# Moving the fifth bias table of a neighbourhood attention stage behind the first token tile's steps on GpSimd's queue

## The chip, the cores and the metric

One core of one Trainium2 chip runs the whole program. The metric is the device time of one execution in microseconds (us); of the kernel before there are three timed runs and one execution that was taken with a profile. The engines are named as the profile names them: PE is TensorE's matmul side and PEld its weight loads, DVE is VectorE, ACT is ScalarE, POOL is GpSimd, and SP is SyncE, which here only issues transfers.

## What is computed

The reference is an encoder trunk of two layers over 256 tokens of width 1024, in float32:

```python
for layer in range(DEPTH):                     # DEPTH = 2
    x = x + 0.5 * swiglu(rms_norm(x, ffn1_norm[layer]), ...)
    h = rms_norm(x, mix_norm[layer])
    x = x + (even_mixer(h, ...) if layer % 2 == 0 else odd_mixer(h, w_qkv, rel_bias, w_out, rows))
    x = x + 0.5 * swiglu(rms_norm(x, ffn2_norm[layer]), ...)
return rms_norm(x, final_norm)
```

The change lies in the odd mixer of the second layer. It projects to queries, keys and values of 16 heads of 64, and each token attends to a window of its neighbours on a grid of 4 rows by 64 columns. A learned bias, `rel_bias`, which depends on the head and on the two offsets of row and column, is added to the scores ahead of the softmax, and positions outside the window get minus 1e30.

## The kernel before, in words

**Stages.** The program runs six stages one after the other: a feed-forward stage, the even mixer, two feed-forward stages, the odd mixer (`odd`, line 1085), and a last feed-forward stage. The 256 tokens are two tiles of 128 (`tt` 0 and 1). Weights come from memory in units of up to 1 MB by SP (`load`, line 312) into three raw buffers. ACT rounds each piece to a high part (`hi`, line 415), DVE takes the rest as a low part (`lo`, line 418), and PE makes three matmuls for each pair of pieces: high by high (line 407), low by high (line 408) and high by low (line 409). When both parts of a raw buffer have been made, SP's next transfer into it may start.

**How the order comes about.** Each engine carries out its instructions in the order in which the program writes them. The program writes the matmuls of the main loop, and behind each set of three it calls `tick` (line 232). A tick resumes the side tasks whose countdown has run out. A side task is a generator that writes some instructions, for any engine, and yields the number of ticks to its next piece. So a `yield` costs nothing on the chip by itself: it only decides where in the queues of the engines the next instructions stand.

**The odd mixer.** It works on two groups of eight heads. For each group the main loop projects keys, then queries, then values, for both token tiles. The results pass through these tasks:

- `natural` (line 1097) scales a projection on ACT (`nat`, line 1105; for queries DVE first makes the factor `rs`, line 1103) and has PE turn it into `tp` (`turned`, line 484).
- `stack_q` (line 496) writes the turned queries: high parts on ACT and low parts on DVE, both into `oqT`.
- `stack_k` (line 507) does the same for the keys of one token tile: high parts on ACT into `okTz`, low parts on DVE into half the partitions of `okTx`, and a copy of the high parts by POOL into the other half of `okTx` (the CAST of line 514). `okTz` and `okTx` exist twice, for head 0 and head 1 of each pair. Their other halves are cleared by POOL's memsets (line 521), which `keys_tiles` writes when a group begins.
- `attend` (line 762) takes a group's heads in steps `(tt, b0, s)`: tile 0 with `b0` 0 and 2 and `s` 0 and 1, then tile 1. A step writes the scores on PE (`scores`, lines 830 and 831; line 831 reads `okTx`), then DVE adds the bias table and takes the maximum (line 848), ACT makes the exponentials (line 872), DVE normalises (lines 884 and 886), PE turns the result (line 894), and after two steps PE weighs the values (line 815). A score takes all 256 keys, so it needs the keys of both token tiles.

**Bias tables.** `bias_tables` (line 1065) makes eight tables on POOL, one for each two heads, four to a group; the table of number `n` is made in two halves (line 1077) out of rows of `rel_bias` that SP has fetched (`fetch_row`, line 1051). Four row buffers exist, filled for tables 0 to 3 in the stage before; the rows of table `n + 4` are asked for behind table `n`, when its buffer is free. So the rows of the fifth table, `n` = 4, are asked for on SP's queue, which also carries the weights. Five table buffers exist, hence the `while`: table `n` from 5 on may only be written when the four steps that read table `n - 5` have been written. `read` counts these steps as the program writes them. `BIAS_GAP` is the number of ticks behind each half, 0 for tables 0 to 3 and 3 for the others; a number up to 1 means the next tick.

Of the kernel before, what the change touches and what calls it, by code (L numbers as in the profile page):

```python
# [166 lines left out]
class Trunk:  # L167
# [897 lines left out]
    def bias_tables(self, rel, tables, read):  # L1065

        nc = self.nc
        yield BIAS_WAIT
        for n in range(8):
            while n >= 5 and read[n - 5] < 4:  # L1070
                yield 1
            bias = self.t([P, 2, 6, GRID_W], "bias", 5)
            for i in range(2):
                row = self.rows[n][:, i, :]
                runs = bass.AP(row.tensor, row.offset, [row.ap[0], [31, 6], [1, GRID_W]])
                near = self.near.unsqueeze(1).to_broadcast([P, 6, GRID_W])
                nc.gpsimd.tensor_tensor(bias[:, i], runs, near, op=ALU.add)
                if i == 0:
                    yield BIAS_GAP[n // 4]
            tables.append(bias)  # L1080
            if n + ROWS < 8:
                self.fetch_row(rel, n + ROWS)
            yield BIAS_GAP[n // 4]
# [239 lines left out]
```

## Time and profile before

| | us |
|---|---|
| three timed runs | 972.93, 973.35, 974.29 |
| median of these | 973.35 |
| the execution that was profiled | 974.63 |
| its span, from the first to the last instruction | 972.8 |
| PE busy in the span | 954.3 |
| DVE busy | 694.8 |
| ACT busy | 557.2 |
| POOL busy | 88.2 |

The mean granted clock of TensorE over the span is 0.995 of full speed. The odd mixer takes the stretch from some 655 to some 785 us of the span. In a row of the timeline the first number is the start in us, the second the duration, then engine, line, operation and tile; what stands in brackets is how long the engine had been idle just before and what ended that. A row with a count above 1 is merged out of several instructions that follow each other on the engine, and its second number is the time from the first start to the last end. A matmul's duration is modelled and longer than its share of the pipeline; the distance from one start to the next says what it cost.

### The profile page before, as it was taken

What the parts mean: (1) busy time and instruction counts of PE and PEld (TensorE: products, weight loads), DVE (VectorE), ACT (ScalarE), POOL (GpSimd) and SP (SyncE); (2) the same over time, 40 slices, a digit from 0 to 9 for tenths busy, and PEclk for the clock granted to TensorE, in tenths of its full rate; (3) what the DMA queues carried; (4) which work ended last, traced back from release to release, by engine and by line L of the source; (5) the groups of instructions that cost most, each with busy time, mean ns of one, the idle gap of its engine ahead of it and who ended that gap; (6) DMA issues with size and microseconds to landing.
All of it is one profiled execution on the core that took longest, in us unless ns stands there. A gap on an engine that the chain in (4) does not pass through costs nothing.

```text
span 972.8 us, 12839 instructions
## 1 busy us (share of the span) xinstructions
PE 954.3 (98%) x4803; PEld 806.5 (83%) x4803; DVE 694.8 (71%) x1104; ACT 557.2 (57%) x965; POOL 88.2 (9%) x152
## 2 busy tenths in 40 slices
PE   9999999999999999999999999999899999999997
PEld 6888998877778889988888899887678788889886
DVE  5665679778966665787755558788577776655987
ACT  7554556477776544554645546556677575545551
POOL 1030000063410000000000000004230000000002
PEclk9999999999999999999999999999899999999999
DMA  8565555644326645557465465655333456555641
GB/s 271 197 240 187 178 212 181 209 130 106 112 91 218 212 152 159 209 217 255 135 215 193 139 210 189 216 178 187 106 130 130 130 180 210 183 155 182 212 172 71
DMA packets 82367, 171.64 MB, mean 176 GB/s; under 512 B 3712, under 2 KB 25216, under 8 KB 82304
## 3 DMA queue, kind: packets, MB, share of 16 engines
q1 hardware_dynamic: 81728, 170.23, 52.7%
q8 instruction: 37, 0.61, 0.3%
q10 hardware_dynamic: 576, 0.59, 0.2%
q14 instruction: 26, 0.21, 0.1%
HBM read 169.76 MB, written 1.05 MB: 176 GB/s over the span
## 4 chain that ended last, share of the span: by engine, by line
PE 89%; DVE 4%; ACT 2%; DMA 1%; POOL 1%; issue 1%; POOLq 0%; SPq 0%; ACTq 0%; DVEq 0%
PE pj L407 14%; PE pj L409 13%; PE pj L408 13%; PE s L409 11%; PE s L407 11%; PE s L408 11%; PE tp L484 3%; PE o L815 2%; PE o L408 1%; PE o L407 1%; PE o L409 1%; DVE lo L418 1%; PE tp L894 1%; PE tp L462 1%; PE s L830 1%
## 5 line engine op out<-in xcount | busy, mean ns | idle before, releaser
L418 DVE TENSOR_TENSOR lo<-raw,hi 128x1024 fp32r<-128x1024 f32 (+2 forms) x388 | 382.5, 1009 | 121.7 <-ACT hi L415 118.3
L415 ACT ACTIVATE hi<-raw 128x1024 fp32r<-128x1024 f32 (+2 forms) x388 | 327.9, 877 | 148.0 <-PE pj L409 103.9
L407 PE MATMUL pj<-hi,th 128*128 128x512 f32 (+1 forms) x512 | 198.8, 388 | 0.0
L409 PE MATMUL pj<-hi,tl 128*128 128x512 f32 (+1 forms) x512 | 193.6, 378 | 0.0
L408 PE MATMUL pj<-lo,th 128*128 128x512 f32 (+1 forms) x512 | 193.3, 378 | 0.1
L407 PE MATMUL s<-hi,th 128*128 128x512 f32 (+1 forms) x400 | 152.5, 381 | 0.0
L409 PE MATMUL s<-hi,tl 128*128 128x512 f32 (+1 forms) x400 | 149.8, 374 | 0.0
L408 PE MATMUL s<-lo,th 128*128 128x512 f32 (+1 forms) x400 | 149.5, 374 | 0.0
L409 PEld LDWEIGHTS pj<-hi,tl 128*128 128x128 f32 x512 | 96.5, 188 | 15.6
L407 PEld LDWEIGHTS pj<-hi,th 128*128 128x128 f32 x512 | 96.8, 189 | 13.9 <-issue 0.9
L408 PEld LDWEIGHTS pj<-lo,th 128*128 128x128 f32 x512 | 96.8, 189 | 13.5 <-DVE lo L418 0.5
L409 PEld LDWEIGHTS s<-hi,tl 128*128 128x128 f32 x400 | 75.5, 189 | 11.1
L408 PEld LDWEIGHTS s<-lo,th 128*128 128x128 f32 x400 | 75.6, 189 | 10.6
L407 PEld LDWEIGHTS s<-hi,th 128*128 128x128 f32 x400 | 75.7, 189 | 10.3
L599 DVE SCALAR_TENSOR_TENSOR glu<-pj,rstd,silu 128x512 f32<-128x512 f32 (+1 forms) x48 | 33.7, 701 | 36.8 <-PE pj L409 36.6
L418 DVE TENSOR_TENSOR g_l<-tp,g_h 128x384 fp32r<-128x384 f32 (+1 forms) x48 | 29.0, 604 | 22.2 <-ACT g_h L415 22.2
L427 POOL TENSOR_TENSOR rstd<-var,mhalf 128x1 f32<-128x1 f32 (+2 forms) x16 | 15.2, 948 | 312.6 <-DVE var L425 312.5
L447 ACT ACTIVATE th<-tp,mats 128x128 fp32r<-128x128 f32 x88 | 25.1, 371 | 31.3 <-PE tp L462 27.0
L407 PE MATMUL s<-hi,g_h 128*128 128x512 f32 (+1 forms) x108 | 42.8, 396 | 0.0
L409 PE MATMUL s<-hi,g_l 128*128 128x512 f32 (+1 forms) x108 | 42.0, 389 | 0.0
L415 ACT ACTIVATE g_h<-tp 128x384 fp32r<-128x384 f32 (+1 forms) x48 | 25.3, 526 | 29.1 <-PE tp L484 19.0
L408 PE MATMUL s<-lo,g_h 128*128 128x512 f32 (+1 forms) x108 | 41.9, 388 | 0.0
(378 smaller groups left out, 1383.1 us busy)
## 6 DMA issues: line engine op xcount, KB each, us to landing
raw<-in_ffn_w_down SPq DMA_DIRECT2D x44, 1024.0 KB, 5.0
raw<-in_ffn_w_up SPq DMA_DIRECT2D x32, 1024.0 KB, 5.2
raw<-in_ffn_w_gate SPq DMA_DIRECT2D x30, 1024.0 KB, 5.1
raw<-in_ffn_w_gate SPq DMA_DIRECT2D x16, 768.0 KB, 4.5
raw<-in_ffn_w_up SPq DMA_DIRECT2D x16, 768.0 KB, 4.7
raw<-in_odd_w_qkv SPq DMA_DIRECT2D x12, 1024.0 KB, 5.2
raw<-in_even_w_in SPq DMA_DIRECT2D x4, 1024.0 KB, 5.0
raw<-in_even_w_out SPq DMA_DIRECT2D x8, 512.0 KB, 5.7
```

The lines of the kernel that those rows point to most:

```text
L407: mm(ps, h, wh, start=first, stop=False)
L408: mm(ps, h, wl, start=False, stop=False)
L409: mm(ps, l, wh, start=False, stop=last)
L415: self.nc.scalar.activation(hi, src, AF.Copy)
L418: self.nc.vector.tensor_tensor(lo, src, hi.bitcast(F32), op=ALU.subtract)
L427: nc.gpsimd.tensor_tensor(r[:, :n], v[:, :n], self.mhalf[:, :n], op=ALU.pow)
L447: self.nc.scalar.activation(hi, tb[:, j * P : j * P + P], AF.Copy, scale=gain)
L462: nc.tensor.transpose(tb[:, j * P : (j + 1) * P], self.x[tt][:, b * P : (b + 1) * P], self.ident)
L484: self.nc.tensor.transpose(tb[:, i * P : (i + 1) * P], src[:, i * P : (i + 1) * P], self.ident)
L599: nc.vector.scalar_tensor_tensor(m[:, :w], u[:, :w], self.now.r[tt], s[:, :w], op0=ALU.mult, op1=ALU.mult)
L815: self.nc.tensor.matmul(O[64 * s : 64 * s + 64, i * P : i * P + P], v(b0 + i, s, kc), pT[s][:, i, kc, :], start=(kc == 0), stop=(kc == 1),)
L830: nc.tensor.matmul(S[:, i, :], q, kz[s], start=True, stop=False)
```

## The change

```diff
         nc = self.nc
         yield BIAS_WAIT
         for n in range(8):
-            while n >= 5 and read[n - 5] < 4:
+
+            while n >= 5 and read[n - 5] < 4 or n == 4 and read[1] < 2:
                 yield 1
             bias = self.t([P, 2, 6, GRID_W], "bias", 5)
             for i in range(2):
```

The fifth table is now written only when two steps that read table 1 have been written. Table 1 belongs to the second two heads of the first group's first steps; its first two readers are the steps `(0, 0, 0)` and `(0, 0, 1)`, those of token tile 0. Tables 5 to 7 keep their condition. One line is added ahead of it, so lines from 1071 on have a number larger by one.

On POOL the piece of the queue in which the fifth table stands reads as follows in the kernel before. `bias_6383` is the fourth table and `bias_6408` the fifth, made from `rows_6316`; the first two casts copy the keys of token tile 0 and the next two those of token tile 1; the memsets belong to the second group, and `bias_6819` is the sixth table.

```order
L427 TENSOR_TENSOR rstd_6389<-var_6387,mhalf_82 128x1
L1077 TENSOR_TENSOR bias_6383<-rows_5365,mats 128x384
L1077 TENSOR_TENSOR bias_6408<-rows_6316,mats 128x384
L514 CAST okTx_1466_6256<-okTz_1464_6254 64x4x128
L514 CAST okTx_1467_6257<-okTz_1465_6255 64x4x128
L1077 TENSOR_TENSOR bias_6408<-rows_6316,mats 128x384
L514 CAST okTx_1466_6256<-okTz_1464_6254 64x4x128
L514 CAST okTx_1467_6257<-okTz_1465_6255 64x4x128
L521 MEMSET okTz_1572_6693 64x1024
L521 MEMSET okTz_1573_6694 64x1024
L1077 TENSOR_TENSOR bias_6819<-rows_6335,mats 128x384 x2
```

In the changed kernel the same piece of POOL's queue is this, the fifth table being `bias_6653` now:

```order
L427 TENSOR_TENSOR rstd_6389<-var_6387,mhalf_82 128x1
L1078 TENSOR_TENSOR bias_6383<-rows_5365,mats 128x384
L514 CAST okTx_1466_6256<-okTz_1464_6254 64x4x128
L514 CAST okTx_1467_6257<-okTz_1465_6255 64x4x128
L514 CAST okTx_1466_6256<-okTz_1464_6254 64x4x128
L514 CAST okTx_1467_6257<-okTz_1465_6255 64x4x128
L1078 TENSOR_TENSOR bias_6653<-rows_6316,mats 128x384 x2
L521 MEMSET okTz_1572_6693 64x1024
L521 MEMSET okTz_1573_6694 64x1024
L1078 TENSOR_TENSOR bias_6819<-rows_6335,mats 128x384 x2
```

Both halves of the fifth table have moved behind all four casts and still stand ahead of the second group's memsets. Nothing else has moved on POOL, and PE, DVE, ACT and SP have the same instructions in the same order as before; the fifth table issues no transfer of its own.

On PE, unchanged, the first score (four matmuls of lines 830 and 831, of which the second is the first to read `okTx`) stands behind the query projection of token tile 1 and ahead of the value projection of tile 0; behind the first nine matmuls of that value projection stand the four that turn the queries of tile 1 (line 484).

## The prediction

> **What bounds the kernel now.** I read the page first, then who waited for whom on PE, then the clock in stretches around the longest wait, then the timeline of that place engine by engine.
>
> ```profile
> span 972.8 us, 12839 instructions
> PE 89%; DVE 4%; ACT 2%; DMA 1%; POOL 1%; issue 1%; POOLq 0%; SPq 0%; ACTq 0%; DVEq 0%
> ```
>
> The chain that ended last is PE's for 89% of the span, so the kernel is bound by PE, and what makes it shorter is either less PE work or less waiting by PE. The change removes no work. So the question is where PE waits:
>
> ```profile
> PE s L831 <- POOL okTx L514: 5.3, 1, 5.3
> PE o L1246 <- DVE zeros L1244: 1.5, 1, 1.5
> ```
>
> These are the two longest waits of PE in the whole execution. The first is one wait of 5.3 us: the first score of the odd mixer waits for POOL's cast. It is also followed by slow matmuls; in the stretches below the value behind the POOL column is the granted clock, a share of full speed.
>
> ```profile
> 679.40:685.20 5.80, 0.50 (x2) 0.19 (x1) 2.18 (x5) 1.72 (x3) 4.12 (x5) 0.87 0.31 60
> 685.20:690.10 4.90, 4.90 (x14) 3.92 (x15) 1.56 (x6) 0.00 (x0) 2.50 (x3) 0.50 0.87 279
> ```
>
> PE is busy for 0.50 us of the first 5.80, and in the 4.90 us behind it the clock stands at 0.50. Why POOL is late, its own timeline shows, with two pieces of the chain of waits behind it:
>
> ```profile
> 667.60 0.94 POOL L1077 TENSOR_TENSOR bias<-rows,mats 128x384 f32<-128x384 f32 x1
> 680.76 0.93 POOL L1077 TENSOR_TENSOR bias<-rows,mats 128x384 f32<-128x384 f32 x1 [12.21 <-DMA rows<-in_c_rel_bias]
> 681.75 1.72 POOL L514 CAST okTx<-okTz 64x512 fp32r<-64x512 f32 x2
> 683.55 0.93 POOL L1077 TENSOR_TENSOR bias<-rows,mats 128x384 f32<-128x384 f32 x1
> 684.54 1.27 POOL L514 CAST okTx<-okTz 64x512 fp32r<-64x512 f32 x2
> 685.87 1.95 POOL L521 MEMSET okTz<- 64x1024 f32 x2
> ```
>
> ```profile
> 674.62 0.61 SPq L1057
> 675.28 5.34 DMA rows<-in_c_rel_bias
> ```
>
> POOL has ended the fourth table at 668.54 (667.60 and 0.94). The next in its queue is the first half of the fifth, whose rows SP asks for only at 674.62 and which land 5.34 us on. So POOL stands idle for 12.21 us with the casts queued behind. Then a half, two casts, the other half, two casts; the first of the last two ends at 685.15 and PE starts at 685.20.
>
> **The change, part by part.** It removes and adds nothing. Two halves of 0.93 us go past four casts, on POOL alone; the fifth table asks for no rows, so SP's queue is as before.
>
> *When the casts run now.* They need the keys' high parts from ACT, of which those of tile 1 are the later:
>
> ```profile
> 670.22 1.21 ACT L415 ACTIVATE okTz<-tp 64x512 fp32r<-64x512 f32 x2 [1.21 <-PE tp L484]
> ```
>
> Tile 1's are there at 671.43. Tile 0's stand well ahead of them in ACT's queue, so its two casts (1.27 us) start when POOL is free, at some 668.6, and end by 669.9. How fast casts follow, the second group's keys show, where nothing is ahead of them:
>
> ```profile
> 713.64 1.21 ACT L415 ACTIVATE okTz<-tp 64x512 fp32r<-64x512 f32 x2 [2.02 <-PE tp L484]
> 714.36 1.28 POOL L514 CAST okTx<-okTz 64x512 fp32r<-64x512 f32 x2 [3.60 <-ACT okTz L415]
> 714.88 1.39 DVE L418 TENSOR_TENSOR okTx<-tp,okTz 64x512 fp32r<-64x512 f32 x2 [2.20 <-ACT okTz L415]
> ```
>
> The casts end 2.00 us after ACT's start, so at 672.22 here. PE reaches the score at 679.59: POOL is 7 us early, and the wait goes.
>
> *What is late next at the score.* It also needs DVE's low parts of the queries, the first at 678.76, two in 1.41 us:
>
> ```profile
> 678.76 1.41 DVE L418 TENSOR_TENSOR oqT<-tp,oqT 64x512 fp32r<-64x512 f32 x2
> 679.59 0.36 PE L830 MATMUL s<-okTz,oqT 128*128 128x256 f32 x1
> 685.20 0.58 PE L831 MATMUL s<-okTx,oqT 128*128 128x256 f32 x1 [5.26 <-POOL okTx L514]
> 689.85 0.95 PE L484 MATMUL tp<-mats,nat 128*128 128x128 f32 x4
> 690.55 0.48 PE L407 MATMUL pj<-hi,th 128*128 128x512 f32 x1
> ```
>
> That start at 679.59 stays. From it to 690.55 PE needs 10.96 us for four score matmuls, nine of the value projection and four that turn the queries of tile 1. Undisturbed, the same work costs what it does elsewhere in this stage:
>
> ```profile
> 693.42 0.28 PE L830 MATMUL s<-okTz,oqT 128*128 128x256 f32 x1
> 693.89 0.40 PE L407 MATMUL pj<-hi,th 128*128 128x512 f32 x1
> 695.96 0.39 PE L407 MATMUL pj<-hi,th 128*128 128x512 f32 x1
> ...
> 669.58 0.60 PE L484 MATMUL tp<-mats,nat 128*128 128x128 f32 x4
> 669.94 0.48 PE L407 MATMUL pj<-hi,th 128*128 128x512 f32 x1
> ```
>
> Start to start that is 0.47 for a score, 2.07 for nine matmuls (three sets lie between 693.89 and 695.96) and 0.36 for the turning, 2.90 together. So 10.96 - 2.90 = 8.06 us are to be had. Of these, 685.20 - 679.59 - 0.12 = 5.49 are the wait itself (0.12 being a quarter of 0.47), and the other 2.57 the slow clock.
>
> [...]
>
> *Whether the rest follows.* Behind the score, the next that PE needs from others is `nat` of the queries of tile 1, and the next that others need from PE is its turning:
>
> ```profile
> 681.07 0.69 ACT L1105 ACTIVATE nat<-pj,rs 128x512 f32<-128x512 f32 x1 [2.54 <-DVE rs L1103]
> 681.65 1.14 ACT L415 ACTIVATE hi<-raw 128x512 fp32r<-128x512 f32 x2
> 690.84 0.59 ACT L415 ACTIVATE oqT<-tp 64x512 fp32r<-64x512 f32 x1 [8.04 <-PE tp L484]
> ```
>
> PE now comes to the turning at 679.59 + 0.47 + 2.07 = 682.13, and `nat` ends at 681.76: 0.37 us to spare. ACT is through with its two pieces at 682.79 and then idled 8.04 us for PE, so its whole later queue comes forward by about as much as PE. On DVE the first score's maximum comes forward less:
>
> ```profile
> 682.31 0.69 DVE L418 TENSOR_TENSOR lo<-raw,hi 128x512 fp32r<-128x512 f32 x1 [1.35 <-ACT hi L415]
> ...
> 686.25 0.42 DVE L848 CUSTOM_DVE_ANT_1 p<-s,bias 128x256 f32<-128x256 f32 x1 [3.25 <-PE s L831]
> ```
>
> It starts at 683.0, behind that low part, 3.2 us earlier and not 8. Two maxima (about 0.9) and a low part (0.69) behind it end at 684.6, while ACT's parts of the queries of tile 1 are there at 682.8 + 1.2 = 684.0. So DVE is 0.6 us later against PE than before. PE doesn't read these queries before the scores of tile 1, over 20 matmuls on.
>
> The weights: one transfer starts at a time that does not move, all later ones are released by DVE's low parts, which come forward too.
>
> ```profile
> 683.03 0.37 SPq L322 DMA_DIRECT2D raw<-in_odd_w_qkv  x1
> ...
> 697.61 0.37 SPq L322 DMA_DIRECT2D raw<-in_odd_w_qkv  x1
> raw<-in_odd_w_qkv SPq DMA_DIRECT2D x12, 1024.0 KB, 5.2
> ```
>
> The first lands at about 683.03 + 5.2 = 688.2. Of the three raw buffers, the one that SP got at 697.61 held a unit two ahead of it, so its own first piece was split later than that; with 8 us off, later than 689.6. It is there in time.
>
> *What the move costs.* POOL's casts at 668.6 now run beside DVE's low parts of the weights. DVE, in the stretch in which POOL made tables (658.5 to 668.5) and in the one in which it stood idle (668.5 to 680.5):
>
> ```profile
> L418 DVE TENSOR_TENSOR lo<-raw,hi 128x512 fp32r<-128x512 f32 x5 | 5.7, 1165 | 0.3 <-ACT hi L415 0.3
> ...
> L418 DVE TENSOR_TENSOR lo<-raw,hi 128x512 fp32r<-128x512 f32 x8 | 5.3, 690 | 3.2 <-ACT hi L415 3.1
> ```
>
> A low part beside POOL's work took 0.475 us longer. Three of them stand where the first casts go:
>
> ```profile
> 668.56 1.90 DVE L418 TENSOR_TENSOR lo<-raw,hi 128x512 fp32r<-128x512 f32 x3
> 671.46 1.39 DVE L418 TENSOR_TENSOR okTx<-tp,okTz 64x512 fp32r<-64x512 f32 x2 [1.00 <-ACT okTz L415]
> ```
>
> At worst 3 x 0.475 = 1.43, of which DVE's idle 1.00 takes most; 0.43 is left, and it could go through `rs`, `nat` and the turning to the score at 679.59. At best nothing, since the casts last 1.3 us and not 1.9. The second pair of casts meets the keys' low parts, which take 1.39 us at 714.88 with casts beside them and 1.39 at 671.46 without. A gain by less contention later is possible as well, since the memsets leave 685.87; it would be off PE's path. I take 0.15.
>
> [...]
>
> The fifth table itself ends at 680.76 + 1.9 = 682.7, and the memsets at 684.7 (1.95 behind it), ahead of the 687.8 of before. Group 2 needs the memsets at 713.64 - 8 = 705.6, and reads the fifth table later still. Both are covered by over 20 us.
>
> **The sum.** 8.06 - 0.15 = 7.9 us. The profiled execution of 974.63 us (its span and 1.83 around it) becomes 966.7. It lies 1.28 above the median of the runs, 973.35, from which the same gain gives 965.5.
>
> **The rivals.** *Only the wait goes.* The runs without a profile lie up to 1.7 us below the profiled one; where the rows land sooner or the slow clock does not set in, there is less to gain. Then 5.49 less up to 0.43, so some 5.1 to 5.5 us: 968.0. The 0.50 over 4.90 us speaks against it.
>
> *A new wait takes part of the place.* `nat` has 0.37 us to spare and hangs on DVE's `rs`, behind queries' low parts that have none. If DVE runs late by one table half beside it (0.93) at two steps, PE waits up to 1.9 us less 0.37 there: 973.35 - 7.9 + 1.5 = 967.0. The half at 680.76 stands in the same place in both kernels, which speaks against it.
>
> *No change.* The score's wait was inferred from semaphores. Were it DVE's or the row transfer's own, the order on POOL would not matter: 973.4. The cast that ends at 685.15 and the start at 685.20 speak against it.
>
> *Slower.* The fifth table now stands directly ahead of the second group's memsets. If its rows came late, the memsets, then ACT's keys of the second group, then PE would wait. That costs PE something once the memsets end after 705.6, so when the rows land 21 us later than they did, and it makes the kernel slower by 2 us once they land 31 us later: 975.4. In the profile they took 5.34 us.
>
> **How the numbers follow.** The full gain has 0.72; its own range is 7.0 to 8.6 us, with half a microsecond for the median of other runs, 964.7 to 966.4. Only the wait 0.16, a new wait 0.05, no change 0.04, slower 0.03. Low end: 8.06 and about 1 for the scatter of the runs (972.93 to 974.29) gives 964.3. High end: the wait alone less contention and half a microsecond of scatter, 4.5, gives 968.9. What a measurement can tell from no change is about 0.2%, 1.95 us; the first three cases pass it: faster 0.93, same 0.04, slower 0.03.
>
> **What would show it.** In the profile of the changed kernel: no wait of PE for `okTx`; four casts ended by 673, both halves of the fifth table behind them from some 680.8; no stretch at clock 0.50 near 685; ACT's idle of 8.04 ahead of `oqT` under 0.5; a span of about 964.9. I am wrong if PE still waits over 1 us between 679 and 684, or if the 8 us come back as waits before the stage ends.

## The result, and the profile after

The changed kernel takes 965.62 us in the median (965.20 to 966.42 in four runs); the kernel before, with one more run beside its three from above, 973.14 (972.89 to 974.29). The ratio is 0.9921, with a 95% interval of 0.9904 to 0.9939: faster by some 7.5 us. The predicted time was 965.5.

From the page of the changed kernel and from what PE waited for, the longest first:

```profile
span 963.4 us, 12838 instructions
```

```profile
PE o L1247 <- DVE zeros L1245: 1.4, 1, 1.4
PE tp L970 <- POOL kra L923: 1.0, 1, 1.0
```

The wait of 5.3 us that headed this list is gone, and no other came in: what led behind it leads now. The two stretches that showed the idle PE and the slow clock, by the same columns as before:

```profile
679.40:685.20 5.80, 5.80 (x31) 4.87 (x30) 4.32 (x12) 5.45 (x10) 3.65 (x4) 1.00 0.37 118
685.20:690.10 4.90, 4.90 (x27) 4.20 (x26) 4.20 (x15) 4.87 (x12) 0.00 (x0) 1.00 0.69 189
```

PE is busy throughout and the clock stands at 1.00. POOL's queue at that place:

```profile
666.15 0.94 POOL L1078 TENSOR_TENSOR bias<-rows,mats 128x384 f32<-128x384 f32 x1
667.15 3.82 POOL L514 CAST okTx<-okTz 64x512 fp32r<-64x512 f32 x4
679.25 1.91 POOL L1078 TENSOR_TENSOR bias<-rows,mats 128x384 f32<-128x384 f32 x2 [8.27 <-DMA rows<-in_c_rel_bias]
681.21 1.95 POOL L521 MEMSET okTz<- 64x1024 f32 x2
```

All four casts have ended by 670.97. POOL still waits 8.27 us for the rows of the fifth table, but nothing that PE needs stands behind it. PE at the first score, up to the first matmul behind the turning of the second queries:

```profile
678.14 0.35 PE L830 MATMUL s<-okTz,oqT 128*128 128x256 f32 x1
678.33 0.28 PE L831 MATMUL s<-okTx,oqT 128*128 128x256 f32 x1
678.68 0.40 PE L407 MATMUL pj<-hi,th 128*128 128x512 f32 x1
...
680.77 0.60 PE L484 MATMUL tp<-mats,nat 128*128 128x128 f32 x4
681.13 0.48 PE L407 MATMUL pj<-hi,th 128*128 128x512 f32 x1
```

The score starts 1.45 us earlier in this execution than in that of before (679.59), and so does everything ahead of it: the fourth table's last half starts at 666.15 against 667.60. That offset is older than the place of the change. From the score to the last row PE took 681.13 - 678.14 = 2.99 us, where it had taken 10.96. So 7.97 us went here, and with the offset that is the whole difference of the two spans, 972.8 - 963.4 = 9.4. Nothing was given back later: from these last rows to the end of the span it is 282.27 us after and 282.25 before. By the medians the gain is 7.5 us and not 7.97; single runs of one kernel lie over 1 us apart.

### The profile page after: what moved, and what is told of

The parts are those of the page before. It is cut to its first block, busy times and chain, and to the rows that moved or that the text cites. A ratio compares the mean times of both kernels' runs of the same rounds, so it can differ in the third digit from the quotient of the medians.

```text
span 963.4 us, 12838 instructions
## 1 busy us (share of the span) xinstructions
PE 950.2 (99%) x4803; PEld 803.6 (83%) x4803; DVE 696.2 (72%) x1104; ACT 557.4 (58%) x965; POOL 87.5 (9%) x152
## 4 chain that ended last, share of the span: by engine, by line
PE 91%; DVE 4%; ACT 2%; POOL 1%; issue 1%; DMA 1%; POOLq 0%; ACTq 0%; DVEq 0%
PE pj L407 14%; PE pj L409 14%; PE pj L408 14%; PE s L407 12%; PE s L409 12%; PE s L408 11%; PE tp L484 3%; PE o L815 2%; PE o L409 1%; PE o L407 1%; PE o L408 1%; PE tp L894 1%; DVE lo L418 1%; PE tp L462 1%; PE s L830 1%
```

## The experiments

Each was timed beside the kernel before. In the three sessions that one had medians of 973.61, 973.34 and 973.60.

### The slow clock by itself

PE gets 22 matmuls that nobody reads, directly ahead of the first score of the kernel before. They use the high parts of the main loop's last set once more, which `mm` notes for them:

```diff
+        self.recent = lh[0], piece
...
+            if tag == "ot0_" and (tt, b0, s) == (0, 0, 0):
+                h, piece = self.recent
+                o = self.bank("o")
+                for _ in range(22):
+                    nc.tensor.matmul(o, h, piece.split.parts[0][:, piece.i, :], start=True, stop=True)
             S = self.scores(tt, b0, s, qT(tt), kT, sink is not None)
```

> The kernel before, with 22 extra matmuls on PE directly ahead of the odd mixer's first score; they write a free PSUM bank that nothing reads, so they only keep PE busy through most of its wait for POOL's casts (22 x 0.23 = 5.0 us of the 5.5). Theory (5.49 us of the 8 are the wait, 2.57 the slow clock behind it): the wait ends when it did, but the clock stays full, so 973.1 - 2.5 = 970.6 us, and no stretch at clock 0.50. Rival (the slow clock costs nothing by itself, or doesn't come from PE's idleness): 973.1, with the slow stretch still there or PE waiting for somebody else in its place.

Measured: 971.14 us, a ratio of 0.9974 (0.9965 to 0.9983), so 2.5 us less with more work. PE in this run (line numbers are larger by 1 to 6; 837 is the score's second matmul, 408 the first of a set):

```profile
678.41 5.15 PE L780 MATMUL o<-hi,th 128*128 128x512 f32 x22
683.40 0.28 PE L836 MATMUL s<-okTz,oqT 128*128 128x256 f32 x1
684.25 0.39 PE L837 MATMUL s<-okTx,oqT 128*128 128x256 f32 x1 [0.58 <-POOL okTx L515]
...
684.72 0.40 PE L408 MATMUL pj<-hi,th 128*128 128x512 f32 x1
684.95 0.40 PE L409 MATMUL pj<-lo,th 128*128 128x512 f32 x1
```

The casts come when they came before, and PE goes on no sooner; but its matmuls follow at 0.23 us behind the wait and not at 0.43. In the profile PE takes 2.89 us from the end of the wait to the first matmul behind the turning (684.25 to 687.14), where it had taken 5.35 (685.20 to 690.55). The slow clock was 2.5 of the 8 us, as the sum had it (2.57), and PE's own idleness made it.

### The wait, without moving anything

The kernel before with its order, but with the fifth table made from the fourth table's rows, which have long landed. So this kernel leaves out the fifth table's own values:

```diff
-                row = self.rows[n][:, i, :]
+                row = self.rows[3 if n == 4 else n][:, i, :]
...
-            if n + ROWS < 8:
+            if n + ROWS < 7:
                 self.fetch_row(rel, n + ROWS)
+            if n == 4:
+                self.fetch_row(rel, 7)
```

> The kernel before with its order on POOL untouched, but the fifth table is made from the fourth table's rows, which have long landed (so its values are not those of the reference); the fourth row buffer is refilled behind it. Theory (what costs is that the casts queue behind a table that waits for its rows, not the 1.9 us of the table itself): POOL no longer stands idle, the casts end by about 674, 5 us ahead of the score at 679.6, and the time is that of the change, 965.6 us. [...]

Measured: 966.52 us, 0.9928 (0.9914 to 0.9942). POOL, DVE and PE in this run:

```profile
667.42 1.84 POOL L1077 TENSOR_TENSOR bias<-rows,mats 128x384 f32<-128x384 f32 x2
669.33 1.98 POOL L514 CAST okTx<-okTz 64x512 fp32r<-64x512 f32 x2
671.38 1.27 POOL L1077 TENSOR_TENSOR bias<-rows,mats 128x384 f32<-128x384 f32 x1
672.72 1.73 POOL L514 CAST okTx<-okTz 64x512 fp32r<-64x512 f32 x2
```

```profile
668.38 3.47 DVE L418 TENSOR_TENSOR lo<-raw,hi 128x512 fp32r<-128x512 f32 x3
```

```profile
675.91 0.66 PE L484 MATMUL tp<-mats,nat 128*128 128x128 f32 x4 [0.42 <-ACT nat L1107]
```

With the table where it stood, but no wait for its rows, the casts end at 674.45 and the score does not wait. So the wait for the rows ahead of the casts was the cost, not the table's 1.9 us. The median lies 0.9 us above the changed kernel's, with intervals that overlap. The profile shows 0.42 us of it that the change doesn't have: POOL works beside DVE longer, the three low parts take 3.47 us, `nat` comes late, and PE waits for it.

### One half only

```diff
                 if i == 0:
                     yield BIAS_GAP[n // 4]
+                while i == 0 and n == 4 and read[1] < 2:
+                    yield 1
```

> The kernel before with only the second half of the fifth table moved behind the casts; the first half stays ahead of them and waits for its rows. Theory: the casts start at 681.75 as before, and the third follows the second directly, so PE's wait ends about 1.1 us sooner (684.1 in place of 685.2) and is still long enough for the slow clock: 972.0 us. Rival (it is the half between the two pairs of casts that holds them up): near 965.6. Rival (a wait of 4.4 us no longer slows the clock): 969.5.

Measured: 972.51 us, 0.9990 (0.9981 to 0.9999). In its trace:

```profile
680.91 3.08 POOL L514 CAST okTx<-okTz 64x512 fp32r<-64x512 f32 x4
```

```profile
678.75 0.36 PE L830 MATMUL s<-okTz,oqT 128*128 128x256 f32 x1
683.36 0.58 PE L831 MATMUL s<-okTx,oqT 128*128 128x256 f32 x1 [4.26 <-POOL okTx L514]
...
688.72 0.52 PE L407 MATMUL pj<-hi,th 128*128 128x512 f32 x1
```

The wait is 4.26 in place of 5.26 us, the clock still falls (the nine matmuls behind the score follow at 0.43 us), and the piece from the score on takes 9.97 us, 0.99 less than before. As long as one half that waits for rows stands ahead of the casts, nearly all of the cost stays.

### The rival on the slower side

The changed kernel, with the rows of tables 4 to 7 asked for only when the fifth table is written:

```diff
+            if n == 4:
+                for late in range(ROWS, 8):
+                    self.fetch_row(rel, late)
             bias = self.t([P, 2, 6, GRID_W], "bias", 5)
...
-            if n + ROWS < 8:
-                self.fetch_row(rel, n + ROWS)
```

> The changed kernel with the rows of tables 4 to 7 asked for only when the fifth table is written, which on SP's queue is behind a unit of weights issued at about 712 in the changed kernel: the fifth table's rows come some 39 us later and land near 718. The prediction's rival for a slower kernel says that ACT's keys of the second group wait for the memsets behind the fifth table: memsets end near 722, needed at 704, so PE stands over 10 us and the time is about 978 to 982 us. Other theory: ACT writes the half of okTz that the memsets don't, so ACT goes on, and only POOL's casts of the second group stand behind; their reader on PE, the second group's first score, comes near 729, and the casts end near 728: 965.6 to 967 us.

Measured: 967.17 us, 0.9934 (0.9920 to 0.9948). POOL's fifth table, its last casts of the second group and the reader of these on PE:

```profile
719.36 2.29 POOL L1081 TENSOR_TENSOR bias<-rows,mats 128x384 f32<-128x384 f32 x2 [47.20 <-DMA rows<-in_c_rel_bias]
...
729.59 1.97 POOL L514 CAST okTx<-okTz 64x512 fp32r<-64x512 f32 x2
```

```profile
730.59 0.39 PE L831 MATMUL s<-okTx,oqT 128*128 128x256 f32 x1 [0.94 <-POOL okTx L514]
```

The table comes 40 us later than in the changed kernel (679.25), and PE waits 0.94 us, at the second group's first score. The median lies 1.5 us above the changed kernel's in the other session; this wait is 0.94 of that, and what made the rest stays open. ACT's keys of the second group did not wait for the memsets, which start at 721.70: ACT wrote these keys at 705.35 and 714.80, and its longest wait ahead of them was for PE, 2.0 us, as in the changed kernel.

### How early the casts are, and what a shorter wait costs

The changed kernel was run again in the session of the next three, and then with extra work on POOL between the casts of tile 0 and those of tile 1: `n` memsets, or twelve additions of 240 columns with both inputs in SBUF. The sixth call of `stack_k` is the one for the keys of tile 1 in the odd mixer's first group, which is what `keyed == 6` picks.

```diff
         yield 1
+        self.keyed = getattr(self, "keyed", 0) + 1
+        if self.keyed == 6:
+            extra = self.t([P, 512], "extra")
+            for _ in range(n):
+                self.nc.gpsimd.memset(extra, 0.0)
         for s in range(2):
             self.nc.gpsimd.tensor_copy(X[s]
```

> The changed kernel once more, beside the next three, so that they have it on the same chip: 965.6 to 966.5 us, about 0.992 of the kernel before.

> The changed kernel with 14 extra memsets (128x512, which nothing reads) on POOL between the casts of token tile 0 and those of tile 1: some 14 x 0.53 = 7.4 us by the 1.95 us that two memsets of 1024 took. Theory (the casts are over 7 us early for the score, and POOL's writing alone doesn't hold DVE up): the first cast of tile 1 ends near 677.4, ahead of the score at 678.3, and the time is that of the changed kernel within 0.5 us. Rival (the slack is smaller than worked out, or DVE is held up beside memsets): 1 to 3 us more.

> As the run with 14 memsets, with 21, some 11.1 us: the first cast of tile 1 ends near 681, so PE waits about 2.8 us at the first score. Theory (a wait of 4.3 us halved the clock, one of this length doesn't): 2.8 us over the changed kernel and no stretch at clock 0.50. Rival (any wait of some us brings the slow clock): 5.3 us over it.

> As the run with 14 memsets, but with 12 additions (128x240, both inputs from SBUF) in their place, some 12 x 0.65 = 7.8 us, so also short of the score by their length alone. Theory (POOL's instructions that read SBUF block DVE's low parts of the weights, which have two inputs there): the low parts between 669 and 677 take 1.0 to 1.3 us each in place of 0.69, DVE's queue runs late, nat and the queries' low parts with it, and PE waits 1 to 2 us more than in the changed kernel. Rival (what POOL does matters only by its length): the time of the run with 14 memsets.

> The changed kernel with 16 extra memsets on POOL between the two pairs of casts. In the run with 14 the first cast of tile 1 came some 0.2 us ahead of the score, and a memset took 0.58 us, so PE waits about 0.9 us here. [...]

> With 17 memsets PE waits about 1.5 us. [...]

> With 19 memsets PE waits about 2.7 us. [...]

| run | median us | ratio to before (95%) | PE's wait at the score | slow matmuls behind it |
|---|---|---|---|---|
| changed kernel again | 965.67 | 0.9922 (0.9905 to 0.9938) | none | none |
| 14 memsets | 965.63 | 0.9921 (0.9906 to 0.9935) | none | none |
| 16 memsets | 967.30 | 0.9938 (0.9924 to 0.9953) | 0.76 | none |
| 17 memsets | 967.09 | 0.9936 (0.9920 to 0.9953) | 1.47 | none |
| 12 additions | 968.81 | 0.9955 (0.9940 to 0.9969) | 1.62 | yes |
| 19 memsets | 970.34 | 0.9966 (0.9953 to 0.9979) | 2.49 | yes |
| 21 memsets | 971.72 | 0.9981 (0.9972 to 0.9991) | 3.64 | yes |

With 14 memsets POOL is busy right up to the score:

```profile
669.66 8.11 POOL L517 MEMSET extra<- 128x512 f32 x14
677.83 1.28 POOL L519 CAST okTx<-okTz 64x512 fp32r<-64x512 f32 x2
```

```profile
678.76 0.28 PE L836 MATMUL s<-okTx,oqT 128*128 128x256 f32 x1
```

Eight microseconds of POOL work fit ahead of the second casts without any cost, as the sum said that they are some 7 us early. The memsets were longer than I had put them, 0.58 and not 0.53 us, so the run with 21 had a wait of 3.64 and not 2.8 and left open whether a wait as short as 2.8 slows the clock. The run with 19 tells it:

```profile
681.92 0.38 PE L836 MATMUL s<-okTx,oqT 128*128 128x256 f32 x1 [2.49 <-POOL okTx L519]
...
682.61 0.48 PE L408 MATMUL pj<-lo,th 128*128 128x512 f32 x1
682.88 0.63 PE L409 MATMUL pj<-hi,tl 128*128 128x512 f32 x1
...
685.87 0.76 PE L484 MATMUL tp<-mats,nat 128*128 128x128 f32 x4
686.39 0.48 PE L407 MATMUL pj<-hi,th 128*128 128x512 f32 x1
```

Behind a wait of 2.49 us the first matmuls still run at full speed; then, at 682.78 by the trace's record of the granted clock, it falls, and at 686.19 it is back. From 682.38, where the first set starts, to 686.39 that makes 4.01 us for what takes 2.43 undisturbed (2.07 and 0.36): the slow clock costs 1.6, with the wait 4.1 of the 4.7 us that the medians differ by. The rest is scatter from ahead of the stage: the run with 16 memsets, of which 965.6 + 0.9 = 966.5 was to be expected, reached its score 0.9 us later in the profile than the changed kernel in the session before, with a wait of 0.76. The run with 17 came out at 967.09 us, between 966.59 and 967.26, which is the changed kernel's 965.67 and the wait of 1.47, and its profile has no slow matmuls: behind the wait they follow at 0.23 us. So the clock fell after a wait of 2.49 us and not after one of 1.47.

With the additions the expectation was half right. The two low parts behind the first three, first in the run with 14 memsets and then in that with the additions:

```profile
671.86 1.29 DVE L418 TENSOR_TENSOR lo<-raw,hi 128x512 fp32r<-128x512 f32 x2
```

```profile
671.38 1.71 DVE L418 TENSOR_TENSOR lo<-raw,hi 128x512 fp32r<-128x512 f32 x2
```

POOL and PE in the run with the additions:

```profile
669.32 9.74 POOL L517 TENSOR_TENSOR extra<-mats 128x240 f32<-128x240 f32 x12
```

```profile
680.13 0.39 PE L836 MATMUL s<-okTx,oqT 128*128 128x256 f32 x1 [1.62 <-POOL okTx L519]
...
680.62 0.63 PE L407 MATMUL pj<-hi,th 128*128 128x512 f32 x1
...
684.00 0.39 PE L409 MATMUL pj<-hi,tl 128*128 128x512 f32 x1
```

Beside memsets the same two low parts took 1.29 us, beside additions 1.71: DVE is held up by the one kind and not by the other, but by 0.2 us for each of these low parts and not by the 0.3 to 0.6 expected. PE's wait was again for the casts, and not, as expected, for `nat` or the queries' low parts; that it lies in the expected 1 to 2 us is luck. The casts came late because the additions took 0.81 us each on average and not 0.65. The single additions show why: seven of the twelve take 0.59 us, and the next follows 0.66 behind their start, as expected; the other five take 0.91 to 1.13, and each of these five, and none of the seven, starts while a low part of the weights runs on DVE. That makes 1.9 us in all, more than PE's wait of 1.62. So here lying side by side cost POOL more, 1.9 us, than DVE, some 0.2 for a low part, and through POOL's casts it reached PE. The wait cost twice its length, 3.1 us between the medians, since 1.62 us were enough for the slow clock here.

## Why the prediction was right

*The wait and its cause.* The casts stood behind a table that waited for its rows. The wait went when the order was changed, and as well when the order was left and the rows were there. That the casts are some 7 us early held too.

*The slow clock.* 2.57 us were put on it; the extra matmuls alone won 2.5. By the trace's record of the granted clock that of the kernel before stood at 0.50 from 683.73 to 690.56, so PE worked at half speed from the end of its wait to the last row that the sum counted. The rival that only the wait goes is out by this.

*The sum.* 8.06 us were to be had at this place, 7.97 came, in a profile whose offset of 1.45 us at the start of the place makes the span 963.4 and not 964.9. By the medians it was less, 7.5 us and in the later session 7.7 (973.34 - 965.67), against the 7.9 of the forecast. That the time was met to 0.1 us is in part luck, since the new median of the kernel before lies 0.2 below the one that the forecast started from.

*POOL beside DVE.* I had taken 0.15 us off for POOL's casts beside DVE. They did hold DVE up, by 0.83 us, under the 1.43 that the text put at worst and within DVE's idle 1.00, and it cost nothing:

```profile
667.10 2.73 DVE L418 TENSOR_TENSOR lo<-raw,hi 128x512 fp32r<-128x512 f32 x3
670.00 1.39 DVE L418 TENSOR_TENSOR okTx<-tp,okTz 64x512 fp32r<-64x512 f32 x2 [0.18 <-ACT okTz L415]
...
677.31 1.41 DVE L418 TENSOR_TENSOR oqT<-tp,oqT 64x512 fp32r<-64x512 f32 x2
```

The three took 2.73 in place of 1.90 us, and DVE's idle time behind them shrank from 1.00 to 0.18. Nor did the first two casts last 1.3 us: they took 2.1 beside the low parts (667.15 to 669.28), since the two engines held up each other. So 0.83 of the slack of 1.00 was used, and the queries' low parts start 0.83 ahead of the score as before. It was nearer than the 0.15 sounds: in the run with old rows, where the table's halves lie there as well, the slack did not do, and PE waited 0.42 us. Not all that POOL does holds DVE up: two low parts took 1.71 us beside additions and 1.29 beside memsets, and in the changed kernel, with POOL idle, the same two take 1.29 us as well. A gain from the memsets' move to another time, which the prediction held possible, is thus not to be expected.

*What follows behind the score.* ACT's queue came forward whole, without the idle time of 8.04 us:

```profile
679.62 0.69 ACT L1106 ACTIVATE nat<-pj,rs 128x512 f32<-128x512 f32 x1 [2.55 <-DVE rs L1104]
680.21 1.14 ACT L415 ACTIVATE hi<-raw 128x512 fp32r<-128x512 f32 x2
681.41 1.20 ACT L415 ACTIVATE oqT<-tp 64x512 fp32r<-64x512 f32 x2
```

`nat` ends at 680.31 and PE turns it from 680.77, 0.46 to spare where 0.37 was forecast. DVE ends what stands ahead of the second queries' low parts at 683.31, 0.7 us behind ACT's high parts (682.61); 0.6 was forecast.

*What was wrong.* The rival on the slower side had its price wrong. It said that ACT's keys of the second group need the memsets, so that rows 21 us late would cost time and rows 31 us late make the kernel slower by 2 us. With the table 40 us later PE waited 0.94 us. ACT writes the half of `okTz` that the memsets don't, so it goes on; only the casts stand behind the table, and the score that reads them comes 50 us behind the first group's (728.21 against 678.14 in the changed kernel). The kernel was far safer on that side than the text made it.

## What to carry to other kernels

A helper engine that works through its queue in order should not have work that waits for a transfer ahead of work that the bound engine waits for: here 12.21 us of POOL's idle time ahead of the casts became 5.26 us of PE's. Moving the first behind the second cost PE no wait here, and 0.94 us when the moved work came 40 us later still. A wait of the matmul engine is to be priced with the slow matmuls behind it: here 5.5 us of waiting cost 8, a wait of 1.62 cost twice its length, and one of 1.47 its length alone. Before such a move, count what the moved instructions now lie beside: here they used 0.83 of 1.00 us of another engine's slack.

## What the runs showed of the hardware

The clock fell after waits much shorter than 5 us. The profiles in the order of PE's wait at the score, with the distance from one start to the next in the nine matmuls behind the score, and the time from the end of the wait to the first matmul behind the turning:

| run | wait, us | start to start, us | end of the wait to that matmul, us |
|---|---|---|---|
| 16 memsets | 0.76 | 0.23 | 2.89 |
| 17 memsets | 1.47 | 0.23 | 2.87 |
| 12 additions | 1.62 | 0.43, from 684.00 on 0.23 | 4.45 |
| 19 memsets | 2.49 | 0.23, from 682.88 on 0.43 | 4.47 |
| 21 memsets | 3.64 | 0.43, from 687.12 on 0.23 | 4.46 |
| one half moved | 4.26 | 0.43 | 5.36 |
| before | 5.26 | 0.43 | 5.35 |

The trace records when the granted clock changed. In the kernel before it stood at 0.50 for 6.83 us, from 683.73 to 690.56, with 19 memsets for 3.41 us, from 682.78 to 686.19, and with the additions for 3.41 us from 680.53 on. Here are those 3.41 us, by the columns of before (PE's busy time stands behind the length, the clock behind POOL), and ahead of them the same piece of the run with 17 memsets, where the clock held:

```profile
680.48:683.89 3.41, 3.41 (x20) 2.86 (x19) 2.76 (x7) 1.64 (x4) 3.27 (x4) 1.00 0.15 13
```

```profile
680.53:683.94 3.41, 3.41 (x10) 2.74 (x10) 2.85 (x7) 0.98 (x2) 3.27 (x4) 0.50 0.15 25
```

This also says what a wait cost on top of its length. With the additions and with 19 memsets PE was at work again when the clock fell, 0.40 and 0.86 us behind the end of the wait, and the slow clock cost 1.6 us: 4.45 and 4.47 against the 2.87 of the run with 17 memsets. In the kernel before the clock fell 1.47 us ahead of the end of the wait, so PE was slow from there to the turning, which makes 5.35, so 2.5 for the clock. With one half moved it was the same, 5.36.

These are waits at one place of one program, with one profile of each kernel. By what rule the clock falls, and how little idle time brings the full clock back, these runs leave open.
